# A gated mixer layer on one core: sums of the projections moved from GpSimd to VectorE, and the residual written into the result banks before the output products

## The chip, the cores and the metric

The kernel runs on one core of one Trainium2 chip. A core has TensorE (PE: matrix products out of SBUF into eight PSUM banks of 128 x 512 f32), VectorE (DVE), ScalarE (ACT), GpSimd (POOL) and SyncE (SP, which only issues transfers here). Each engine works through its own queue in order; semaphores connect them. The metric is the device time in microseconds.

## The reference

One layer over 512 tokens of width 1024. What matters here:

```python
h = x @ w_in[i]
ua, va, za, qh, kh, vh, zb, ga, gb = jnp.split(h, IN_OFFSETS, axis=-1)
...
ya = ua * sa.reshape(bn, s_len, A_WIDTH) * jax.nn.silu(za)
...
yb = o.reshape(bn, s_len, B_WIDTH) * jax.nn.silu(zb)
merged = jax.nn.sigmoid(ga) * (ya @ w_branch_a[i]) + jax.nn.sigmoid(gb) * (yb @ w_branch_b[i])
mix_out = merged @ w_out[i]
ple = jax.nn.sigmoid(x @ w_ple_gate[i]) * (p[i] @ w_ple[i])
x = layer_norm(DEEPNORM_ALPHA * x + mix_out + ple, ln_g[i], ln_b[i])
```

`DEEPNORM_ALPHA` is the fourth root of 2, `ALPHA` in the kernel. `w_in`, `w_branch_a`, `w_branch_b`, `w_out` and `w_ple_gate` have 1024 rows, `w_ple` has 256.

## The kernel before

**Products.** An f32 operand is split into a high part (fp32r) and the rest: `h` is a ScalarE copy, `l` is VectorE's `x - h`. Such a pair of operations is called a cut. Each f32 product is then three TensorE products, `three` (L291): high times high, high times low, low times high. A weight unit is 128 x 1024; it is loaded into `wr`, cut into `wh` (L409, ACT) and `wl` (L412, DVE), of which four pairs of buffers rotate.

**Stages.** The projections run one after the other: those of the attention branch first, with the attention beside them, then `ua`, `za`, `va`, `zq`, `ga`, `gb`, `pg` (the embedding's gate), `ple` (the embedding), `wb`, `wa` (the two branch projections) and the output. `va` to `pg`, `wb` and `wa` go through `quad` (L649), which does a 1024 x 1024 product over 2 x 2 blocks with seven block products in place of eight. Its left operand is needed in seven forms: quarters `11`, `12`, `22` and four sums of quarters that the code calls S1, S2, S3 and N4 (a quarter is 512 features by 256 tokens, a tile of 128 x 1024; S1 = 21 - 22, S3 = 11 - 21, S2 = 22 - 11, N4 = S2 + 12). The weights are summed in the same way, by accumulating transfers that POOL issues (L384, in `follow`) when a unit has been cut, or beforehand in memory (`ws_...`). A quad has seven steps of 24 products, in three pairs of banks X, Y and Z. After a step, `after1` to `after7` and `block` (L662) combine banks with ACT copies and DVE subtractions and call the stage's `done`.

**The order around the change.** There is no scheduler. `product` (L279) counts products, and `later(n, fn)` puts `fn` into the program n products further on. Each engine's queue has the order in which such calls fall due; an engine does not wait for a product unless a semaphore says so. The numbers in lines 80 to 92 are such distances: `YB...` and `YA...` say when the quarters and sums of `yb` and `ya` are made and cut, in halves (`in_parts`: two numbers for two halves of 128 x 512). The sums are made by POOL (`add`, L1221 to 1223), the cuts by ACT and DVE (`cut_part`, L1208). `yb`'s are made during `gb` and `pg`, to be there for `wb`; `ya`'s during `pg`, `ple` and `wb`, for `wa`. Their places are the four slots of `ys` (tiles `xsh`, `xsl`), the regions of `xh` and `xl` that `x` no longer needs, and two tiles `yag`, `yab` (`first_sum`) whose room the last norm's gain and shift take later.

**Gates and merge.** `gate_done` (L1195) applies the sigmoid to `ga` and `gb` and stores them in DRAM; `load_gates` brings them back in pairs, through SP, at the distances `GATES`. `mb_done` (L1314) multiplies `wb`'s result by its gate (two of eight pieces on POOL, the others on DVE), `merge` (L1346) does so for `wa` and adds the two (for tokens 0 to 255 on POOL in part). `merge_turn` (L1353) follows at a distance `MERGE`: four TensorE transposes into bank `tr` or `po`, an ACT copy into `xh` and a DVE subtraction into `xl`.

**Embedding, residual and norm.** `base` holds the gate of the embedding, `embed` (L1288) turns it into gate times embedding over `ALPHA`, and `residue` (L1292) adds `x` to it by an accumulating transfer that POOL issues, at the start of the output. The output's first half of the columns is done for two token blocks at a time, with units loaded as it goes, the second half block by block; the last block's second half in two pieces of 256 columns. After each piece `residual` (L1369) adds the bank over `ALPHA` to `base` (DVE) and takes its statistics, and `last_norm` (L1374) normalises and stores; the norm is that of the sum over `ALPHA`, with `EPS` over `ALPHA` squared.

Of the kernel before, what the change touches and what calls it, by code (L numbers as in the profile page):

```python
# [21 lines left out]
P = 128  # L22
# [52 lines left out]

GOES_ON = ('v', 'gb', 'pg', 'wb', 'wa')
# [169 lines left out]
def hybrid_layer(ctx: ExitStack, tc: tile.TileContext, a, out: bass.AP):  # L246
# [402 lines left out]
    def quad(name, left, banks, place, done):  # L649
# [555 lines left out]
    def part_of(tiles, k, t, part):  # L1205
        return (tile[:, 4 * k + 2 * part:4 * k + 2 * part + 2, t * 2 * P:(t + 1) * 2 * P] for tile in tiles)

    def cut_part(source, where, part):  # L1208
        h, l = part_of((xh, xl), *where, part) if where in ((0, 0), (1, 0), (0, 1), (1, 1)) else where(part)
        act.activation(h, source, AF.Copy)  # L1210
        later(CUT_LOW, lambda: dve.tensor_tensor(out=l, in0=source, in1=h.bitcast(F32), op=OP.subtract))

    def cut_yb(k, t, where, part):
        source, = part_of((yb[0],), k, t, part)
        cut_part(source, where, part)

    def cut_ya(k, t, where, part):
        source, = part_of((ua,), k, t, part)
        cut_part(source, where, part)

    def add(tile, to, op, x, y, part):  # L1221
        (z,), (x,), (y,) = (part_of((tile,), *q, part) for q in (to, x, y))
        pool.tensor_tensor(out=z, in0=x, in1=y, op=op)

    def add_ya(*what):
        add(ua, *what)

    def add_yb(*what):
        add(yb[0], *what)
# [6 lines left out]
    def first_sum(part):  # L1236
        if not alone:
            alone.extend(late.tile([P, 4, 2 * P], F32R, name="ya" + n, tag=n) for n in "gb")
        return (tile[:, 2 * part:2 * part + 2, :] for tile in alone)

    def of_first_sum(t, k):
# [25 lines left out]
    in_parts(cut_yb, YB11, 0, 0, (0, 0))  # L1267
    in_parts(cut_yb, YB12, 1, 0, (1, 0))
    in_parts(add_yb, YB_S2, (0, 0), OP.subtract, (1, 1), (0, 0))
    in_parts(add_yb, YB_N4, (1, 0), OP.add, (0, 0), (1, 0))  # L1270
    in_parts(cut_yb, YB_CUT_S1, 1, 1, slot(0))
    in_parts(cut_yb, YB_CUT_N4, 1, 0, slot(2))
    in_parts(cut_yb, YB_CUT_S2, 0, 0, slot(1))
    in_parts(cut_yb, YB_CUT_S3, 0, 1, slot(3))
    in_parts(cut_ya, YA22, 1, 1, (1, 1))
    in_parts(add_ya, YA_S1, (1, 1), OP.subtract, (0, 1), (1, 1))
    in_parts(add_ya, YA_S3, (0, 1), OP.subtract, (0, 0), (0, 1))
    in_parts(cut_ya, YA_CUT_S1, 1, 1, first_sum)
# [49 lines left out]
    in_parts(cut_ya, YA11, 0, 0, (0, 0))  # L1328
    in_parts(cut_ya, YA12, 1, 0, (1, 0))
    in_parts(add_ya, YA_S2, (0, 0), OP.subtract, (1, 1), (0, 0))  # L1330
    in_parts(add_ya, YA_N4, (1, 0), OP.add, (0, 0), (1, 0))
    in_parts(cut_ya, YA_CUT_S3, 0, 1, slot(0))
    in_parts(cut_ya, YA_CUT_N4, 1, 0, slot(2))
    in_parts(cut_ya, YA_CUT_S2, 0, 0, slot(1))
# [11 lines left out]
    def merge(c, t, z, source):  # L1346
        early = t < NT // 2
        by = pool if early and c else dve
        by.tensor_tensor(out=z, in0=source, in1=gate.pop(("ga", c, t)), op=OP.mult)
        (pool if early else dve).tensor_tensor(out=z, in0=z, in1=mb[0][:, t, c * T:(c + 1) * T], op=OP.add)  # L1350
        later(MERGE["early" if early else c], merge_turn, c, t, z)

# [10 lines left out]
    of_ya = [of_first_sum, of_sum(ys, 1), of_sum(ys, 2), of_sum(ys, 0)]  # L1363
    quad("wa", operands(xh, xl, of_ya), pairs(False), lambda c, t: None, merge)


    zst = [small([P, 2 if t < NT - 1 else 3, 6], "vst", 4) for t in range(NT)]

    def residual(t, piece, n, bank):  # L1369
        z = base[:, t, piece * n:(piece + 1) * n]  # L1370
        dve.scalar_tensor_tensor(out=z, in0=bank, scalar=1.0 / ALPHA, in1=z, op0=OP.mult, op1=OP.add)
        dve.bn_stats(out=zst[t][:, piece if n == T else piece - 1, :], in_=z)

    def last_norm(t, cuts):  # L1374
        mv, rs = rstd_of(zst[t], EPS / ALPHA ** 2)
        lg, lb = norm_last
        for c in cuts:
            z = base[:, t, c]
            dve.scalar_tensor_tensor(out=z, in0=z, scalar=mv[:, 0:1], in1=lg[:, c],
                                     op0=OP.subtract, op1=OP.mult)  # L1380
        for c in cuts:
            z = base[:, t, c]
            dve.scalar_tensor_tensor(out=z, in0=z, scalar=rs[:, 0:1], in1=lb[:, c], op0=OP.mult, op1=OP.add)
            sp.dma_start(out=out[t * P:(t + 1) * P, c], in_=z)
# [84 lines left out]
```

## Time and profile before

| what | us |
|---|---|
| median of three runs (lowest, highest) | 621.21 (620.9, 624.6) |
| the profiled execution | 622.56 |
| its span, first to last instruction | 620.8 |
| `pg`: 432.09 to 471.65 | 39.56 |
| `ple`: 471.65 to 482.80 | 11.15 |
| `wb`: 482.80 to 522.38 | 39.58 |
| `wa`: 522.38 to 566.31 | 43.93 |
| output: 566.31 to the last product's end | 47.2 |

Times in the profile count from the first instruction. A row of the timeline has a start, a duration, the engine, the line, the operation, what it writes and reads, how many are merged into it, and in brackets how long the engine had stood still and what ended that. A matmul row's end overlaps the next one's start, so stalls of TensorE are read from start to start. DMA share is the mean busy share of the 16 DMA engines. A tile's name stands without its buffer's number: `ps_pp`, `ps_tx`, `ps_sc`, `ps_tr` and `ps_po` are the banks (three, one, two, one, one).

### The profile page before, as it was taken

How to read it: one execution, taken by the hardware profiler on the slowest of the kernel's cores; microseconds unless marked ns; L12 is line 12 of the kernel's file. 1: busy time of each engine (PE TensorE's matmuls, PEld its weight loads, DVE VectorE, ACT ScalarE, POOL GpSimd, SP SyncE). 2: the span in 40 equal slices, each digit the busy share in tenths (PEclk: the TensorE clock that was granted, in tenths of full speed). 3: DMA queues.
4: the chain of work that ended last, by engine and by line, in shares of the span. 5: the costliest groups of instructions: out<-in, count | busy, mean ns of one | idle time of the engine just before them, and what ended most of it. 6: DMA issues, size and time to landing. Idle time of an engine off the chain costs nothing.

```text
span 620.8 us, 8616 instructions
## 1 busy us (share of the span) xinstructions
PE 607.7 (98%) x3012; PEld 508.5 (82%) x3012; DVE 470.4 (76%) x778; ACT 338.3 (54%) x542; POOL 156.6 (25%) x156
## 2 busy tenths in 40 slices
PE   9999999999999999999999999999999999998995
PEld 6888888888888888888899988888887787776884
DVE  6995687878888765748578987678799788658476
ACT  6656664645645654478665665546676554543200
POOL 1234011332432630230102121141423152443011
PEclk9999999999999999999999999999999999999998
DMA  8789889679797597668898898967976487999102
GB/s 288 237 242 190 259 288 268 246 188 290 267 255 273 177 295 223 160 183 300 272 311 191 244 226 241 234 173 232 232 205 195 178 235 208 255 224 267 33 34 102
DMA packets 45631, 138.52 MB, mean 223 GB/s; under 512 B 6036, under 2 KB 7188, under 8 KB 45268
## 3 DMA queue, kind: packets, MB, share of 16 engines
q1 hardware_dynamic: 35092, 102.71, 46.4%
q0 software_dynamic: 9920, 34.87, 30.7%
q8 instruction: 24, 0.39, 0.3%
q10 hardware_dynamic: 576, 0.39, 0.2%
q14 instruction: 19, 0.16, 0.1%
HBM read 118.95 MB, written 30.54 MB: 241 GB/s over the span
## 4 chain that ended last, share of the span: by engine, by line
PE 85%; DMA 6%; DVE 4%; issue 3%; ACT 1%; POOL 1%; DVEq 0%; SPq 0%; POOLq 0%; ACTq 0%
PE ps_pp L280 52%; PE ps_sc L280 15%; PE ps_tx L280 6%; PE ps_sc L801 3%; DMA wr<-in_w 3%; PE ps_po L846 3%; DMA gates<-gate_ga 1%; DVE wl L412 1%; PE ps_tr L835 1%; PE ps_po L280 1%; PE ps_tr L280 1%; DMA wr<-ws_wb 1%; DVE base L1290 1%; PE ps_tr L1172 1%; PE ps_po L1172 1%
## 5 line engine op out<-in xcount | busy, mean ns | idle before, releaser
L412 DVE TENSOR_TENSOR wl<-wr,wh 128x1024 fp32r<-128x1024 f32 (+1 forms) x143 | 190.2, 1334 | 45.6 <-ACT wh L409 43.4
L409 ACT ACTIVATE wh<-wr 128x1024 fp32r<-128x1024 f32 (+1 forms) x143 | 147.1, 1033 | 72.9 <-PE ps_sc L280 29.0
L280 PE MATMUL ps_pp<-xh,wh 128*128 128x512 f32 (+1 forms) x276 | 109.3, 397 | 0.0
L280 PE MATMUL ps_pp<-xl,wh 128*128 128x512 f32 (+1 forms) x276 | 107.0, 388 | 0.1
L280 PE MATMUL ps_pp<-xh,wl 128*128 128x512 f32 (+1 forms) x276 | 105.5, 383 | 0.0
L280 PE MATMUL ps_pp<-wh,xh 128*128 128x512 f32 (+1 forms) x168 | 64.0, 381 | 0.3 <-DVE s L665 0.2
L280 PE MATMUL ps_pp<-wh,xl 128*128 128x512 f32 (+1 forms) x168 | 64.2, 382 | 0.0
L280 PE MATMUL ps_pp<-wl,xh 128*128 128x512 f32 (+1 forms) x168 | 64.0, 381 | 0.0
L814 ACT ACTIVATE p<-p,sth 128x128 f32<-128x128 f32 (+3 forms) x64 | 35.5, 556 | 46.6 <-DVE sth L812 46.5
L384 POOL DMA_DIRECT2D wr<-in_w x34 | 29.6, 872 | 122.1 <-DVE wl L412 118.1
L280 PEld LDWEIGHTS ps_pp<-xh,wl 128*128 128x128 f32 x276 | 52.1, 189 | 8.9 <-DVE wl L307 0.2
L280 PEld LDWEIGHTS ps_pp<-xh,wh 128*128 128x128 f32 x276 | 52.0, 189 | 8.5 <-ACT wh L306 0.5
L280 PEld LDWEIGHTS ps_pp<-xl,wh 128*128 128x128 f32 x276 | 52.1, 189 | 8.3 <-DVE xl L307 0.4
L746 POOL TENSOR_TENSOR hl<-m,hl 128x512 fp32r<-128x512 f32 x16 | 25.1, 1627 | 54.4 <-ACT hl L741 54.4
L280 PEld LDWEIGHTS ps_pp<-wh,xh 128*128 128x128 f32 x168 | 31.6, 188 | 7.3 <-DVE s L665 0.6
L280 PEld LDWEIGHTS ps_pp<-wl,xh 128*128 128x128 f32 x168 | 31.6, 188 | 6.2 <-DVE wl L412 0.4
L280 PEld LDWEIGHTS ps_pp<-wh,xl 128*128 128x128 f32 x168 | 31.6, 188 | 5.7
L808 DVE CUSTOM_DVE_ANT_0 p<-ps_sc,mask 128x128 f32<-128x128 f32 (+3 forms) x64 | 30.9, 483 | 6.3 <-PE ps_sc L801 6.3
L280 PE MATMUL ps_sc<-wl,xsh 128*128 128x512 f32 x88 | 34.5, 392 | 0.6 <-DVE wl L412 0.6
L280 PE MATMUL ps_sc<-wh,xsh 128*128 128x512 f32 x88 | 34.3, 390 | 0.0
L280 PE MATMUL ps_sc<-wh,xsl 128*128 128x512 f32 x88 | 34.2, 389 | 0.0
L280 PE MATMUL ps_pp<-wh,xsh 128*128 128x512 f32 x80 | 31.4, 393 | 0.1
(315 smaller groups left out, 1268.1 us busy)
## 6 DMA issues: line engine op xcount, KB each, us to landing
wr<-in_w SPq DMA_DIRECT2D x81, 512.0 KB, 4.7
wr<-in_w POOLq DMA_DIRECT2D x30, 512.0 KB, 6.2
k<-hl SPq DMA_DIRECT2D x16, 256.0 KB, 5.4
q<-hl SPq DMA_DIRECT2D x16, 256.0 KB, 4.1
ws_va<-in_w POOLq DMA_DIRECT2D x8, 512.0 KB, 10.3
wr<-ws_va SPq DMA_DIRECT2D x8, 512.0 KB, 4.3
wa<-in_w POOLq DMA_DIRECT2D x6, 512.0 KB, 7.2
kx<-hl SPq DMA_DIRECT2D x12, 256.0 KB, 5.4
```

Source lines behind the costliest of these rows:

```text
L280: pe.matmul(ps, s, m, start=start, stop=stop, skip_group_check=read_within)
L384: pool.dma_start(out=raw[u][:, :n], in_=weights(STEPS[FOLLOWS[u]][1], n), accum_op=OP.add)
L409: act.activation(h, raw[u][:, :width(STEPS[u][0])], AF.Copy)
L412: dve.tensor_tensor(out=l, in0=raw[u][:, :width(STEPS[u][0])], in1=h.bitcast(F32), op=OP.subtract)
L746: pool.tensor_tensor(out=hl[:, 3 - j, :], in0=m[2 * j], in1=hl[:, j, :].bitcast(F32), op=OP.subtract)
L801: pe.matmul(sc[m][:, :n], q[:, m, i * P:(i + 1) * P], kk[:, m, :n], start=o == 0, stop=o == 1)
L808: dve.tensor_tensor_reduce(out=pr[m][:, :n], in0=sc[m][:, :n], in1=mask[:, T - n:], scale=-(DK ** -0.5), scalar=3e38, op0=OP.add, op1=OP.m ...
L814: act.activation(pr[m][:, :n], pr[m][:, :n], AF.Exp, bias=st[:, m:m + 1], scale=-1.0, accum_out=st[:, 2 + m:3 + m])
L835: pe.transpose(tr[:, j * P:(j + 1) * P], ad[:, j * P:(j + 1) * P], ident)
L846: pe.matmul(po[:, i * P:(i + 1) * P], at[:, j * P:(j + 1) * P], v[:, j, h * P:(h + 1) * P], start=j == 0, stop=j == i)
L1172: pe.matmul(sa[:, t * P:(t + 1) * P], va[:, t, g * P:(g + 1) * P], aux[0][:, 0, g, :], start=True, stop=True)
L1290: dve.scalar_tensor_tensor(out=z, in0=bank, scalar=1.0 / ALPHA, in1=z, op0=OP.mult, op1=OP.mult)
```

## The change

- Quarters are cut whole (`split_quarter`), not in halves. Sums of `yb` stay on POOL in halves (a tuple of two distances in `combine`), as do S1 and S3 of `ya`; S2 and N4 of `ya` go to DVE, whole (a single distance).
- S1 and S3 of `ya`, made in `ple` before (distances 180 to 204 from the start of `pg`), are made in `pg`. Quarter `22` of `ya` is cut in `pg` too, into the two tiles apart; the sum S1 takes the place in `xh` and `xl` that the quarter had, and is cut in `wb`. The cut of `yb`'s S3 falls into `wb`, the cuts of `ya`'s N4 and S2 into `wa`.
- `pT` is loaded and cut earlier in `pg`.
- In `ga`, `gb` and `pg` the sigmoid follows its subtraction by 8 products, not 2.
- All multiplications and additions of `mb_done` and `merge` are DVE's. `MERGE` has a distance for each piece.
- The four transfers that add `x` to `base` are issued in `wb`; the loads of the last norm's gain and shift move from `wa` into the output.
- `fill`: ScalarE writes `ALPHA * base` into a result bank, for nine pieces in eight banks; the output's products start without clearing the bank and accumulate onto it. `residual` falls away: `stats` reads the bank, and the first step of `last_norm` reads it in place of `base`. The norm is that of the sum itself.

```diff
+SIGMOIDS = ('ga', 'gb', 'pg')
-YB22, YB_S1, YB_S3 = (60, 72), (80, 92), (104, 116)
-YB11, YB12, YB_S2, YB_N4 = (26, 33), (50, 57), (46, 58), (70, 82)
-YB_CUT_S1, YB_CUT_N4, YB_CUT_S2, YB_CUT_S3 = (75, 82), (101, 108), (124, 131), (150, 157)
-YA22, YA_S1, YA_S3, YA_CUT_S1 = (170, 177), (180, 188), (196, 204), (200, 207)
-YA11, YA12, YA_S2, YA_N4 = (26, 33), (50, 57), (44, 52), (68, 76)
-YA_CUT_S3, YA_CUT_N4, YA_CUT_S2 = (78, 85), (98, 105), (122, 129)
+YB22, YB_S1, YB_S3 = 60, (80, 92), (104, 116)
+YB11, YB12, YB_S2, YB_N4, YB_SUMS = 25, 49, (34, 46), (58, 70), (75, 101, 124, 226)
+YA22, YA_S1, YA_S3 = 36, (84, 96), (108, 120)
+YA11, YA12, YA_S2, YA_N4, YA_SUMS = 26, 50, 54, 64, (19, 76, 172, 196)
-LAST_NORM = (100, 130)
-MERGE = {'early': 24, 1: 23, 0: 22}
-RESIDUE = (2, 8, 26, 32)
+LAST_NORM = (172, 184)
+MERGE = (36, 36, 25, 27), (40, 40, 68, 62)
+RESIDUE = (10, 34, 58, 82)
+FIRST_FILL = (150, 156)
+FILL = ((14, 0, 1), (20, 2, 0), (24, 1, 1), (30, 3, 0), (136, 2, 1), (160, 3, 1), (164, 3, 2))
...
-            later(2, done, c, t, z, z)
+            later(8 if name in SIGMOIDS else 2, done, c, t, z, z)
...
+    def split_quarter(n, source, where):
+        def high():
+            h, l = where()
+            act.activation(h, source, AF.Copy)
+            later(CUT_LOW, lambda: dve.tensor_tensor(out=l, in0=source, in1=h.bitcast(F32), op=OP.subtract))
+
+        later(n, high)
+
+    def combine(ats, to, op, x, y):
+        def part(engine, e):
+            z, a0, a1 = (q[:, e] for q in (to, x, y))
+            engine.tensor_tensor(out=z, in0=a0, in1=a1, op=op)
+
+        if isinstance(ats, int):
+            later(ats, part, dve, slice(0, 4))
+        else:
+            for i, n in enumerate(ats):
+                later(n, part, pool, slice(2 * i, 2 * i + 2))
...
-            later(40 + 12 * k, cut, phl[0][:, 0, k, :], phl[0][:, 1, k, :], pt)
-
-    later(64, load_p)
+            later(26 + 12 * k, cut, phl[0][:, 0, k, :], phl[0][:, 1, k, :], pt)
+
+    later(34, load_p)
...
-        by = pool if c == 1 and t < 2 else dve
-        by.tensor_tensor(out=z, in0=source, in1=gate.pop(("gb", c, t)), op=OP.mult)
+        dve.tensor_tensor(out=z, in0=source, in1=gate.pop(("gb", c, t)), op=OP.mult)
...
+    for t, n in enumerate(RESIDUE):
+        later(n, residue, t)
...
-        early = t < NT // 2
-        by = pool if early and c else dve
-        by.tensor_tensor(out=z, in0=source, in1=gate.pop(("ga", c, t)), op=OP.mult)
-        (pool if early else dve).tensor_tensor(out=z, in0=z, in1=mb[0][:, t, c * T:(c + 1) * T], op=OP.add)
-        later(MERGE["early" if early else c], merge_turn, c, t, z)
+        dve.tensor_tensor(out=z, in0=source, in1=gate.pop(("ga", c, t)), op=OP.mult)
+        dve.tensor_tensor(out=z, in0=z, in1=mb[0][:, t, c * T:(c + 1) * T], op=OP.add)
+        later(MERGE[c][t], merge_turn, c, t, z)
...
+    last_columns = [[(0, T), (T, D)] for _ in range(NT - 1)] + [[(0, T), (T, T + T // 2), (T + T // 2, D)]]
+    held = {}
+
+    def fill(t, i):
+        c0, c1 = last_columns[t][i]
+        bank = (pbank("sc", 2) if (t < 2 and i == 0) or (t >= 2 and i == 1) else
+                pbank("tx", 1) if t == 2 else pp())
+        held[t, i] = bank[:, :c1 - c0]
+        act.activation(held[t, i], base[:, t, c0:c1], AF.Copy, scale=ALPHA)
+
+    for t in range(2):
+        later(FIRST_FILL[t], fill, t, 0)
...
+    def stats(t, piece, bank):
+        dve.bn_stats(out=zst[t][:, piece, :], in_=bank)
+
+    def last_norm(t, cuts):
+        mv, rs = rstd_of(zst[t])
+        lg, lb = norm_last
+        for i, cs in enumerate(slice(*c) for c in last_columns[t]):
+            dve.scalar_tensor_tensor(out=base[:, t, cs], in0=held[t, i], scalar=mv[:, 0:1], in1=lg[:, cs],
+                                     op0=OP.subtract, op1=OP.mult)
...
-    def residual(t, piece, n, bank):
-        z = base[:, t, piece * n:(piece + 1) * n]
-        dve.scalar_tensor_tensor(out=z, in0=bank, scalar=1.0 / ALPHA, in1=z, op0=OP.mult, op1=OP.add)
-        dve.bn_stats(out=zst[t][:, piece if n == T else piece - 1, :], in_=z)
...
-                three(banks[t], xh[:, k, ts], xl[:, k, ts], h[:, m], l[:, m], k == 0, k == KT - 1)
+                three(held[t, 0], xh[:, k, ts], xl[:, k, ts], h[:, m], l[:, m], False, k == KT - 1, True)
...
-            later(2 + 6 * (t % 2), residual, t, 0, T, banks[t])
+            later(2 + 6 * (t % 2), stats, t, 0, held[t, 0])
```

More of the change, by code (lines that the diff above doesn't have):

```diff
@@ L1138, in hybrid_layer, with rstd_of @@
     later(AUX[4], mask_ws)
-    def rstd_of(st, eps=EPS):
+    def rstd_of(st):
         mv = small([P, 2], "mv")
         dve.bn_aggr(out=mv, in_=st)
-        dve.tensor_scalar(out=mv[:, 1:2], in0=mv[:, 1:2], scalar1=eps, scalar2=None, op0=OP.add)
+        dve.tensor_scalar(out=mv[:, 1:2], in0=mv[:, 1:2], scalar1=EPS, scalar2=None, op0=OP.add)
         rs = small([P, 1], "rs")
@@ L1203, in hybrid_layer @@
     ys = xs
[L1205 to L1229, printed above, removed]
+    def quarter(tile, k, t):
+        return tile[:, 4 * k:4 * k + 4, t * 2 * P:(t + 1) * 2 * P]
+    def natural(k, t):
+        return lambda: (quarter(xh, k, t), quarter(xl, k, t))
@@ L1231, in slot @@
     def slot(c):
-        return lambda part: (tile[:, c, 2 * part:2 * part + 2, :] for tile in ys)
+        return lambda: (ys[0][:, c], ys[1][:, c])
     alone = []
[L1236 to L1241, printed above, removed]
-        return tuple(tile[:, k, t * P:(t + 1) * P] for tile in alone)
-    def in_parts(fn, ats, *what):
-        for part, n in enumerate(ats):
-            later(n, fn, *what, part)
@@ L1248, in hybrid_layer, with apart, of_apart @@
-    in_parts(cut_yb, YB22, 1, 1, (0, 1))
-    in_parts(add_yb, YB_S1, (1, 1), OP.subtract, (0, 1), (1, 1))
-    in_parts(add_yb, YB_S3, (0, 1), OP.subtract, (0, 0), (0, 1))
+    def apart():
+        alone.extend(late.tile([P, 4, 2 * P], F32R, name="ya" + n, tag=n) for n in "gb")
+        return alone
+    def of_apart(t, k):
+        return tuple(tile[:, k, t * P:(t + 1) * P] for tile in alone)
+    def split_quarter(n, source, where):
[4 more added lines that the diff above has]
+        later(n, high)
@@ new lines, in combine @@
+    def combine(ats, to, op, x, y):
[7 more added lines that the diff above has]
+                later(n, part, pool, slice(2 * i, 2 * i + 2))
+    yb11, yb12, yb21, yb22 = (quarter(yb[0], k, t) for t in range(2) for k in range(2))
+    ya11, ya12, ya21, ya22 = (quarter(ua, k, t) for t in range(2) for k in range(2))
@@ L1251, in hybrid_layer @@
+    split_quarter(YB22, yb22, natural(0, 1))
+    combine(YB_S1, yb22, OP.subtract, yb21, yb22)
+    combine(YB_S3, yb21, OP.subtract, yb11, yb21)
     quad("gb", of_x, pairs(True), lambda c, t: None, gate_done("gb"))
@@ L1265, in embedding_gate @@
         act.activation(z, source, AF.Sigmoid)
[L1267 to L1278, printed above, removed]
+    split_quarter(YB11, yb11, natural(0, 0))
+    combine(YB_S2, yb11, OP.subtract, yb22, yb11)
+    split_quarter(YB12, yb12, natural(1, 0))
+    combine(YB_N4, yb12, OP.add, yb11, yb12)
+    for n, source, c in zip(YB_SUMS, (yb22, yb12, yb11, yb21), (0, 2, 1, 3)):
+        split_quarter(n, source, slot(c))
+    split_quarter(YA22, ya22, apart)
+    combine(YA_S1, ya22, OP.subtract, ya21, ya22)
+    combine(YA_S3, ya21, OP.subtract, ya11, ya21)
     quad("pg", of_x, pairs(False), lambda c, t: base[:, t, c * T:(c + 1) * T], embedding_gate)
@@ L1327, in hybrid_layer @@
         later(n, load_gates, *what, i % 2)
[L1328 to L1334, printed above, removed]
+    split_quarter(YA_SUMS[0], ya22, natural(1, 1))
+    split_quarter(YA11, ya11, natural(0, 0))
+    combine(YA_S2, ya11, OP.subtract, ya22, ya11)
+    split_quarter(YA12, ya12, natural(1, 0))
+    combine(YA_N4, ya12, OP.add, ya11, ya12)
+    for n, source, c in zip(YA_SUMS[1:], (ya21, ya12, ya11), (0, 2, 1)):
+        split_quarter(n, source, slot(c))
+    for t, n in enumerate(RESIDUE):
+        later(n, residue, t)
     quad("wb", operands(xh, xl, ys, 0), pairs(True), place_b, mb_done)
@@ L1361, in merge_turn @@
                                            in1=xh[:, at[0], at[1]].bitcast(F32), op=OP.subtract))
-    of_ya = [of_first_sum, of_sum(ys, 1), of_sum(ys, 2), of_sum(ys, 0)]
-    quad("wa", operands(xh, xl, of_ya), pairs(False), lambda c, t: None, merge)
-    zst = [small([P, 2 if t < NT - 1 else 3, 6], "vst", 4) for t in range(NT)]
-    def residual(t, piece, n, bank):
-        z = base[:, t, piece * n:(piece + 1) * n]
-        dve.scalar_tensor_tensor(out=z, in0=bank, scalar=1.0 / ALPHA, in1=z, op0=OP.mult, op1=OP.add)
-        dve.bn_stats(out=zst[t][:, piece if n == T else piece - 1, :], in_=z)
@@ L1374, in last_norm @@
[L1374 to L1384, printed above, removed]
@@ L1386, in hybrid_layer @@
-    for t, n in enumerate(RESIDUE):
-        later(n, residue, t)
+    of_ya = (of_parts(xh, xl, 0, 0), of_parts(xh, xl, 4, 0), of_parts(xh, xl, 4, 2 * P),
+             of_sum(ys, 2), of_sum(ys, 1), of_sum(ys, 0), of_apart)
+    last_columns = [[(0, T), (T, D)] for _ in range(NT - 1)] + [[(0, T), (T, T + T // 2), (T + T // 2, D)]]
[6 more added lines that the diff above has]
+        act.activation(held[t, i], base[:, t, c0:c1], AF.Copy, scale=ALPHA)
@@ new lines, in hybrid_layer @@
+    for t in range(2):
+        later(FIRST_FILL[t], fill, t, 0)
+    quad("wa", of_ya, pairs(False), lambda c, t: None, merge)
+    def stats(t, piece, bank):
[6 more added lines that the diff above has]
+                                     op0=OP.subtract, op1=OP.mult)
+        for cs in cuts:
+            z = base[:, t, cs]
+            dve.scalar_tensor_tensor(out=z, in0=z, scalar=rs[:, 0:1], in1=lb[:, cs], op0=OP.mult, op1=OP.add)
+            sp.dma_start(out=out[t * P:(t + 1) * P, cs], in_=z)
@@ L1388, in hybrid_layer @@
+    zst = [small([P, 2 if t < NT - 1 else 3, 6], "vst", 4) for t in range(NT)]
     units = []
+    for n, t, i in FILL:
+        later(n, fill, t, i)
     for those in ((0, 1), (2, 3)):
-        banks = {t: pbank("sc", 2) for t in those} if those[0] else {0: pp(), 1: pbank("tx", 1)}
         for k in range(KT):
@@ L1413, in hybrid_layer @@
         ts = slice(t * P, (t + 1) * P)
-        n = T if t < NT - 1 else T // 2
-        for j in range(T // n):
-            bank = pp()
+        for i, (c0, c1) in enumerate(last_columns[t][1:], 1):
             for k in range(KT):
@@ L1422, in hybrid_layer @@
                 h, l = units[k // 2]
-                m = slice((k % 2) * T + j * n, (k % 2) * T + (j + 1) * n)
-                three(bank[:, :n], xh[:, k, ts], xl[:, k, ts], h[:, m], l[:, m], k == 0, k == KT - 1)
-            later(1, residual, t, T // n + j, n, bank[:, :n])
+                m = slice((k % 2) * T + c0 - T, (k % 2) * T + c1 - T)
+                three(held[t, i], xh[:, k, ts], xl[:, k, ts], h[:, m], l[:, m], False, k == KT - 1, True)
+            later(1, stats, t, i, held[t, i])
         later(1, last_norm, t, [slice(0, D)] if t < NT - 1 else [slice(0, T), slice(T, D)])
```

## The prediction

> **What bounds the kernel now.** I read the page's engine totals first, then busy time by stage, then the matmuls in order of time. Stages are found by counting matmuls back from the last: 216 for the output, 168 each for `wa`, `wb`, `pg`, 48 for `ple`. The stage rows below are, in order, `pg`, `ple`, `wb`, `wa`, output, tail; columns are length, then busy time of PE, PEld, DVE, ACT, POOL, the granted clock, DMA share, GB/s.
>
> ```profile
> span 620.8 us, 8616 instructions
> PE 607.7 (98%) x3012; PEld 508.5 (82%) x3012; DVE 470.4 (76%) x778; ACT 338.3 (54%) x542; POOL 156.6 (25%) x156
> ```
>
> ```profile
> 432.09:471.65 39.56, 39.52 (x178) 32.27 (x176) 33.82 (x35) 28.46 (x42) 9.79 (x9) 1.00 0.84 220
> 471.65:482.80 11.15, 11.15 (x49) 9.04 (x48) 10.99 (x14) 5.32 (x8) 6.08 (x4) 1.00 0.51 166
> 482.80:522.38 39.58, 38.87 (x169) 31.30 (x168) 32.74 (x35) 22.74 (x30) 13.55 (x10) 1.00 0.67 212
> 522.38:566.31 43.93, 41.80 (x190) 33.04 (x188) 30.26 (x30) 20.18 (x25) 18.88 (x17) 1.00 0.96 245
> 566.31:613.50 47.19, 45.65 (x229) 38.34 (x227) 31.91 (x43) 6.99 (x8) 4.57 (x3) 1.00 0.29 75
> 613.50:620.80 7.30, 0.00 (x0) 0.00 (x0) 3.89 (x8) 0.00 (x0) 0.99 (x1) 0.64 0.35 136
> ```
>
> TensorE is the bound, at clock 1.00 in every stage; the change leaves its products as they are, so only its stalls and the tail can be won. Six starts of matmuls take 1.36 us:
>
> ```profile
> 461.10 0.39 PE L280 MATMUL ps_pp<-wl,xsh 128*128 128x512 f32 x1
> ...
> 461.78 0.39 PE L280 MATMUL ps_pp<-wl,xsh 128*128 128x512 f32 x1
> ...
> 462.46 0.39 PE L280 MATMUL ps_pp<-wl,xsh 128*128 128x512 f32 x1
> ```
>
> That is 0.227 us a product, 38.1 us for 168. So `wb` (39.58) holds 1.5 us of stalls. The larger stalls stand in the matmul rows, with what released them in brackets:
>
> ```profile
> 495.05 0.39 PE L280 MATMUL ps_sc<-wh,xsh 128*128 128x512 f32 x1
> 496.04 0.50 PE L280 MATMUL ps_sc<-wl,xsh 128*128 128x512 f32 x1 [0.60 <-DVE wl L412]
> ...
> 536.09 0.39 PE L280 MATMUL ps_sc<-wh,yag 128*128 128x512 f32 x1
> 537.29 0.66 PE L1356 MATMUL ps_po<-ident,s 128*128 128x128 f32 x4 [0.81 <-POOL s L1350]
> 537.70 0.47 PE L280 MATMUL ps_sc<-wl,yag 128*128 128x512 f32 x1
> ...
> 559.12 0.39 PE L280 MATMUL ps_pp<-wl,xh 128*128 128x512 f32 x1
> 560.53 0.66 PE L1356 MATMUL ps_tr<-ident,s 128*128 128x128 f32 x4 [1.03 <-POOL s L1350]
> ...
> 569.04 0.39 PE L280 MATMUL ps_tx<-wl,xh 128*128 128x512 f32 x1
> 570.94 0.66 PE L1356 MATMUL ps_po<-ident,z 128*128 128x128 f32 x4 [1.51 <-DVE xl L1360]
> ```
>
> Start to start, less one product, these lose 0.76, 0.97, 1.18 and 1.67 us. A set of four transposes itself takes 0.41 (537.29 to 537.70) and a little after it. Of `wa`'s excess (43.93 - 38.1 = 5.8), six such sets are about 2.7 and the two POOL stalls 2.15; the remaining 1.0 I count as small stalls. So 1.5 in `wb`, 3.1 in `wa` and 1.7 in the output make 6.3 us that a perfect version could win, and the tail comes on top.
>
> **The change, part by part.**
>
> *Where POOL stops DVE.* These rows pair a POOL operation with the DVE operation that met it:
>
> ```profile
> 412.26 4.25 POOL L1223 TENSOR_TENSOR yb<-yb 128x512 f32<-128x512 f32 x3
> ...
> 490.48 1.29 POOL L1223 TENSOR_TENSOR ua<-ua 128x512 f32<-128x512 f32 x1 [9.43 <-DVE xl L1211]
> ...
> 535.65 2.81 POOL L1350 TENSOR_TENSOR s<-s,mb 128x512 f32<-128x512 f32 x2
> ```
>
> ```profile
> 412.81 4.79 DVE L412 TENSOR_TENSOR wl<-wr,wh 128x1024 fp32r<-128x1024 f32 x1 [2.26 <-ACT wh L409]
> ...
> 458.49 1.21 DVE L412 TENSOR_TENSOR wl<-wr,wh 128x1024 fp32r<-128x1024 f32 x1
> ...
> 490.60 2.26 DVE L412 TENSOR_TENSOR wl<-wr,wh 128x1024 fp32r<-128x1024 f32 x1 [0.26 <-DMA wr<-ws_wb]
> ...
> 535.89 4.80 DVE L412 TENSOR_TENSOR wl<-wr,wh 128x1024 fp32r<-128x1024 f32 x2
> ```
>
> A weight cut takes 1.21 alone; it waited 1.05 for one POOL half, 2.4 for two in a row (two cuts, 4.80), 3.6 for three in a row. So a half that meets DVE costs it about 1.1 to 1.2.
>
> *wb, gain 1.1.* POOL loses four halves of S2 and N4 of `ya` and two multiplications; DVE gets two whole quarters (1.21 each), the two multiplications, and the cuts of S1 of `ya` and S3 of `yb`, which come from the stages before. The whole cuts of N4 and S2 leave `wb` for `wa`. On DVE that is +2 x 1.21 + 2 x 0.69 + 2 x 1.21 - 2 x 1.21 = +3.8. Against it stand the waits that go:
>
> ```profile
> 482.80:522.38 39.58, 19.28 (x14) 1.00 0.67 212
> ...
> 569.59 0.69 DVE L1350 TENSOR_TENSOR z<-z,mb 128x512 f32<-128x512 f32 x1
> ```
>
> The 14 weight cuts of `wb` take 19.28 in place of 14 x 1.21 = 16.9, so 2.3 goes. DVE's 32.74 of 39.58 becomes about 34.2: covered, but the first 80 products hold most of it. Of the 1.5 us of stalls I leave 0.4.
>
> *wa and the start of the output, gain 4.3.* POOL's adds and multiplications leave, eight operations of 0.69 on DVE in their place, each right behind the subtraction that feeds it. The transposes are put 36 and 40 products behind (24 and 23 before), 12 x 0.227 = 2.7 us more, more than the 0.97 and 1.18. The last stall hangs on this:
>
> ```profile
> 559.80 8.95 DMA gates<-gate_ga
> ```
>
> ```profile
> DMA to landing us min/median/max: 8.2/12.1/15.2
> ```
>
> The second row is the four POOL transfers that add `x` to `base`, issued at 560.4 to 562.1, beside that gate. They move to `wb`, and the loads of the norm's gain and shift (SP) behind `wa`; `wa` at DMA share 0.96 loses most of the crowd. With a gate as early as the DVE merge allows and transposes 25 and 27 products behind, I keep 0.5 of 3.1 + 1.7 = 4.8 for small stalls.
>
> *The transfers in wb, 0.* POOL's queue reaches the first three at once after the embedding gates (its queue is not tied to products), then the accumulating load for the last `wb` step, the fourth transfer, and the next accumulating load. Share 0.67 leaves a third of 39.6 us free, 13 us; the cover is that `wb`'s loads run two steps ahead. If the cover is gone, the second accumulating load lands late: bounds 0 and one transfer's spacing, (15.2 - 8.2)/3 = 2.3.
>
> *The seeds, 0.* Nine ScalarE writes into banks, about 0.6 each by the nearest row, replace nine DVE operations:
>
> ```profile
> 525.30 0.58 ACT L672 ACTIVATE ps_pp<-ps_pp 128x512 f32<-128x512 f32 x1 [1.66 <-PE ps_pp L280]
> ```
>
> ACT is busy 6.99 of 47.19 in the output stage. The seeds of a second use (136, 160, 164) wait for the norm of tokens two blocks earlier; what is queued behind on ACT is only the next seed, each 8 or more products (1.8 us) ahead of its use. Between 0 and 1.8 were the norm late; I take 0, as DVE has less to do there.
>
> *The tail, gain 0.36.*
>
> ```profile
> 613.51 0.42 DVE L1371 SCALAR_TENSOR_TENSOR base<-ps_pp,base 128x256 f32<-128x256 f32 x1 [0.18 <-PE ps_pp L280]
> 613.97 0.43 DVE L1372 BATCH_NORM_STATS2 vst<-base 128x6 f32<-128x256 f32 x1
> ...
> 614.77 1.40 DVE L1379 SCALAR_TENSOR_TENSOR base<-base,mv,ln_g 128x512 f32<-128x512 f32 x2
> ```
>
> The residual goes (start to start 0.46). The two normalising operations become three (512, 256, 256 columns, read from banks): one more start, about 0.1.
>
> *pg, loss 2.0.* Here the change puts four more POOL halves (S1, S3 of `ya`, from `ple`) beside the four of `yb`, and nothing of POOL stands between the last three. For POOL's halves and the weight cuts in `pg`:
>
> ```profile
> 432.09:471.65 39.56, 6.61 (x4) 1.00 0.84 220
> ```
>
> ```profile
> 432.09:471.65 39.56, 21.28 (x14) 1.00 0.84 220
> ```
>
> ```profile
> 452.53 3.09 DVE L412 TENSOR_TENSOR wl<-wr,wh 128x1024 fp32r<-128x1024 f32 x1
> ```
>
> ```profile
> 456.34 0.39 PE L280 MATMUL ps_pp<-wl,xsh 128*128 128x512 f32 x1
> ```
>
> The cuts wait 21.28 - 16.9 = 4.3 for four halves. Four more bring DVE from 33.82 to 38.1 or more of 39.56: no reserve. The fifth step's second cut ends at 455.62 and is first read at 456.34, a margin of 0.7. Ahead of it come one more whole cut (1.21, YA22) and two cuts of `pT` (0.69 each, 44 products earlier), 2.6, less some 0.6 of DVE idle time: 1.3 late. Then three halves in a row (3.6, as at 412.81) meet the sixth step, whose second cut ends at 459.70 and is read at 461.78, margin 2.1 + 1.3: with the 2.0 carried in that is 2.2 late. Some halves will meet DVE operations that read a bank, so between 1.3 and 3.5 in sum I take 2.0. Ends: 0, and the four added halves' 4.3 in full plus 1.3, 5.6. `ple` is relieved, but PE does not stall there.
>
> The Trainium skill, page "SBUF — State Buffer", section "SBUF: two separate sides", says that POOL and a DVE operation with two SBUF inputs share one port pair as an exclusive lock for the whole instruction. By that rule every added half costs its full 1.29 where the cuts' rows give about 1.1; four would be 0.8 more and the sum 618.4, an estimate.
>
> *Edits of one answer, 0.* Quarters cut whole in place of two halves save DVE 0.15 each (2 x 0.68 against 1.21), counted above within the margins. The sigmoids of `ga`, `gb` and `pg` come 8 products behind their subtraction, not 2, so ACT no longer stands still for DVE there; PE had no stall over 0.2 us in these stages, and the gates are read a stage later. `pT` is loaded 30 products earlier, ahead of two weight loads in SP's queue; those run a step ahead, and one 512 KB transfer's time, some 4 us, is the price without that cover. `base` must be whole at product 150 of `wa`; the slowest addition of `x` took 15.2 us and is issued more than 60 us before. Statistics and normalisation read banks in place of SBUF: 0.69 for 512 columns either way (L1371 reads a bank at 0.42 for 256, L1372 SBUF at 0.43), so 0, and with 0.1 an operation on either side it would be 0.3 at the tail.
>
> *Sum:* -1.1 - 4.3 + 0 + 0 - 0.36 + 2.0 = -3.8. The profiled execution took 622.56 (span 620.8 and 1.8 around it), 1.35 above the median 621.21 of three runs. So 618.8 for it, 617.4 as a median.
>
> **The rivals.** *pg stays covered* (0 there): 621.2 - 5.8 = 615.4, and 614.3 if the 0.9 of stalls that I keep goes too. For it: DVE idles before `pg`, and the POOL halves may find it reading banks. Against it: the 0.7 margin. *Slower: DVE falls behind in pg.* All eight halves hold it for about 1.1 each and the lateness passes on whole: 5.6 us there give 621.0, all but 0.2 of the gains cancelled; at 1.29 a half with nothing hidden (8 x 1.29 = 10.3, less the 4.3 that is there already, plus the 1.3 of moved cuts, 7.3) it is 622.7. It decides from 5.8 us in `pg`. For it speaks the cut at 412.81, which took 4.79; against it, that DVE idles 5.7 of `pg`'s 39.56 now. *The crowd moves into wb:* 2.3 lost at its last step, 619.7. *The change doesn't do what it says:* transposes still wait, because the last merge waits for its gate, now behind SP's other loads; then 1.7 stays, 619.1.
>
> **How the numbers follow.** My forecast has 0.45, `pg` covered 0.28, DVE behind 0.12, the crowd in `wb` 0.09, the gate 0.06. 617.4 is the first; its own range is 616 to 619.5. The range of 8 in 10 runs from 614.4 to 622.0. About 1% (6.2 us) is what can be told from no change: faster means below 615.0, half of the second case, 0.14; slower means above 627.4, which none of the cases gives, 0.03 for what I don't see; 0.83 between.
>
> **What would show it.** Right: `wb` below 38.7, `wa` below 41 with four sets of transposes, none of them released by POOL; no residual behind the last matmul; `pg` near 41.5 with gaps at its fifth and sixth steps released by weight cuts of three or more us. Wrong: `pg` at 39.6 or less; a gap at `wb`'s last step ended by a POOL transfer; an output matmul that waits for ACT.

## The result and the profile after

The changed kernel takes 625.3 us (median of 13 runs, 623.72 to 627.65) against 621.88 before (13 runs, 620.23 to 625.14): a ratio of 1.0052, 95% interval 1.0033 to 1.0071. It is half a per cent slower; the prediction was 617.4 with a range up to 622.0. The numbers of the experiments below leave out one execution of e5 that took 675.38 at a granted clock of 0.85.

The profiled execution took 627.2, 1.9 above its median, and its span is 4.7 longer than before. These are its totals, and its stages by the same count of matmuls as before (`pg`, `ple`, `wb`, `wa`, output, tail; the columns are length, then busy time of PE, PEld, DVE, ACT, POOL, the granted clock, DMA share, GB/s).

```profile
span 625.5 us, 8563 instructions
PE 609.7 (97%) x3012; PEld 510.9 (82%) x3012; DVE 465.1 (74%) x769; ACT 341.6 (55%) x537; POOL 133.8 (21%) x144
```

```profile
432.56:477.33 44.77, 41.51 (x177) 33.36 (x176) 37.36 (x30) 28.48 (x36) 15.16 (x12) 0.96 0.74 193
477.33:488.49 11.16, 11.16 (x50) 9.04 (x48) 8.13 (x10) 3.56 (x4) 1.76 (x2) 1.00 0.53 159
488.49:530.81 42.32, 39.29 (x169) 31.31 (x168) 30.38 (x31) 21.43 (x25) 4.57 (x6) 1.00 0.87 244
530.81:572.54 41.73, 40.56 (x185) 32.95 (x184) 31.52 (x36) 21.36 (x27) 5.96 (x7) 1.00 0.91 228
572.54:618.47 45.93, 45.90 (x233) 38.81 (x231) 27.58 (x40) 11.96 (x18) 1.66 (x3) 1.00 0.19 67
618.47:625.50 7.03, 0.00 (x0) 0.00 (x0) 3.58 (x8) 0.00 (x0) 0.55 (x1) 0.70 0.23 89
```

| stage | before | after | difference |
|---|---|---|---|
| up to `pg` | 432.09 | 432.56 | +0.5 |
| `pg` | 39.56 | 44.77 | +5.2 |
| `ple` | 11.15 | 11.16 | 0 |
| `wb` | 39.58 | 42.32 | +2.7 |
| `wa` and output | 91.12 | 87.66 | -3.5 |
| tail | 7.30 | 7.03 | -0.3 |

So the last stages gain a little less than was forecast, and `pg` and `wb` lose twice as much. The stretch ahead of `pg` ends between 431.8 and 432.7 in all the profiles, so its 0.5 tells nothing.

In `pg`, POOL first meets two weight cuts at the fifth step: they take 3.68 in place of 2 x 1.21, and TensorE stands still for 0.7:

```profile
454.76 1.60 POOL L1235 TENSOR_TENSOR ua<-ua 128x512 f32<-128x512 f32 x1
```

```profile
454.91 3.68 DVE L413 TENSOR_TENSOR wl<-wr,wh 128x1024 fp32r<-128x1024 f32 x2
```

```profile
456.59 0.39 PE L281 MATMUL ps_pp<-wh,xsh 128*128 128x512 f32 x1
457.51 0.50 PE L281 MATMUL ps_pp<-wl,xsh 128*128 128x512 f32 x1 [0.53 <-DVE wl L413]
```

Then three POOL halves in a row stand against one VectorE cut. First POOL, then DVE, then ACT, from the timeline of the changed kernel:

```profile
458.37 4.08 POOL L1235 TENSOR_TENSOR ua<-ua 128x512 f32<-128x512 f32 x3
```

```profile
458.51 5.04 DVE L1228 TENSOR_TENSOR xsl<-yb,xsh 128x1024 fp32r<-128x1024 f32 x1
463.47 1.21 DVE L413 TENSOR_TENSOR wl<-wr,wh 128x1024 fp32r<-128x1024 f32 x1
```

```profile
465.32 0.63 ACT L1262 ACTIVATE base<-base 128x512 f32<-128x512 f32 x1 [5.73 <-DVE base L666]
```

The cut takes 5.04 where 1.21 is usual: 3.8 for three halves, 1.28 each. This cut is of a sum that only `wb` reads, but a weight cut stands behind it (463.47), and behind that the subtraction that ACT's sigmoid waits for. ACT's queue stands still for 5.73 us, and a copy that frees a bank for TensorE stands behind the sigmoid and one weight cut. TensorE meets both, first the weight cut, then the copy:

```profile
462.90 0.39 PE L281 MATMUL ps_pp<-wh,xsh 128*128 128x512 f32 x1
464.74 0.50 PE L281 MATMUL ps_pp<-wl,xsh 128*128 128x512 f32 x1 [1.45 <-DVE wl L413]
...
465.77 0.39 PE L281 MATMUL ps_pp<-wh,xsl 128*128 128x512 f32 x1
467.43 0.64 PE L281 MATMUL ps_pp<-wh,xsh 128*128 128x512 f32 x1 [1.27 <-ACT s L661]
467.87 0.63 PE L281 MATMUL ps_pp<-wl,xsh 128*128 128x512 f32 x1
```

Start to start, less 0.23, that is 1.6 and 1.4 lost. From 467.43 the starts stand 0.43 apart instead of 0.23, for nine starts, which costs 1.6 more; the window row of that stretch has the granted clock, 0.53, in its column after the engines:

```profile
467.40:470.90 3.50, 3.47 (x9) 2.72 (x10) 3.49 (x5) 2.40 (x3) 0.00 (x0) 0.53 0.18 46
```

The three stalls and the slow starts, 0.7 + 1.6 + 1.4 + 1.6 = 5.3, are the 5.2 by which `pg` is longer.

In `wb` the transfers of `x` are in the way twice. Early on, the first three delay a gate; the chain of waits names the gate's 10.91 us, and DVE stands still for it:

```profile
488.73 10.91 DMA gates<-gate_gb
```

```profile
499.76 0.69 DVE L1309 TENSOR_TENSOR mb<-ps_pp,gates 128x512 f32<-128x512 f32 x1 [1.64 <-DMA gates<-gate_gb]
```

From there to 507.9 DVE works without a pause, so it stays late, and TensorE waits for two of its weight cuts, 0.7 each time:

```profile
500.73 0.39 PE L281 MATMUL ps_sc<-wh,xsh 128*128 128x512 f32 x1
501.64 0.50 PE L281 MATMUL ps_sc<-wl,xsh 128*128 128x512 f32 x1 [0.52 <-DVE wl L413]
...
507.02 0.39 PE L281 MATMUL ps_sc<-wh,xsh 128*128 128x512 f32 x1
507.92 0.50 PE L281 MATMUL ps_sc<-wl,xsh 128*128 128x512 f32 x1 [0.51 <-DVE wl L413]
```

At the end the fourth (L1287) stands in POOL's queue between the two accumulating weight loads (L385) of the last step. The second of these is the one that ACT, and then TensorE, wait for:

```profile
509.87 0.88 POOL L385 DMA_DIRECT2D wr<-in_w  x1 [20.37 <-DVE wl L413]
510.99 0.89 POOL L1287 DMA_DIRECT2D base<-in_x  x1 [0.25 <-issue]
512.14 0.89 POOL L385 DMA_DIRECT2D wr<-in_w  x1 [0.25 <-DMA wr<-in_w]
```

```profile
524.45 2.95 ACT L410 ACTIVATE wh<-wr 128x1024 fp32r<-128x1024 f32 x3 [5.36 <-DMA wr<-in_w]
```

```profile
523.92 0.39 PE L281 MATMUL ps_pp<-wh,xl 128*128 128x512 f32 x1
525.55 0.51 PE L281 MATMUL ps_pp<-wh,xh 128*128 128x512 f32 x1 [1.25 <-ACT wh L410]
526.82 0.51 PE L281 MATMUL ps_pp<-wl,xh 128*128 128x512 f32 x1 [0.76 <-DVE wl L413]
```

Issued at 512.14, used from 524.45: 12.3 us for a load whose kind landed in 5.4 and 6.4 in this place before. TensorE loses 1.4 and 1.0 by it. And the tail, where the residual is gone and three operations read the banks:

```profile
618.48 0.43 DVE L1374 BATCH_NORM_STATS2 vst<-ps_pp 128x6 f32<-128x256 f32 x1 [1.57 <-PE ps_pp L281]
...
619.29 0.74 DVE L1380 SCALAR_TENSOR_TENSOR base<-ps_pp,mv,ln_g 128x512 f32<-128x512 f32 x1
619.95 0.48 DVE L1380 SCALAR_TENSOR_TENSOR base<-ps_sc,mv,ln_g 128x256 f32<-128x256 f32 x1
620.34 0.48 DVE L1380 SCALAR_TENSOR_TENSOR base<-ps_pp,mv,ln_g 128x256 f32<-128x256 f32 x1
```

### The profile page after: what moved, and what is told of

It is laid out like the page before. It is cut to its first block, busy times and chain, and to the rows that moved or that the text cites. A ratio compares the mean times of both kernels' runs of the same rounds, so it can differ in the third digit from the quotient of the medians.

```text
span 625.5 us, 8563 instructions
## 1 busy us (share of the span) xinstructions
PE 609.7 (97%) x3012; PEld 510.9 (82%) x3012; DVE 465.1 (74%) x769; ACT 341.6 (55%) x537; POOL 133.8 (21%) x144
## 4 chain that ended last, share of the span: by engine, by line
PE 84%; issue 5%; DMA 5%; DVE 4%; ACT 1%; POOL 0%; DVEq 0%; POOLq 0%; ACTq 0%; SPq 0%
PE ps_pp L281 50%; PE ps_sc L281 15%; PE ps_tx L281 7%; DMA wr<-in_w 3%; PE ps_sc L802 3%; PE ps_po L847 3%; DMA gates<-gate_gb 2%; PE ps_tr L836 1%; DVE wl L413 1%; PE ps_po L281 1%; PE ps_tr L281 1%; DVE xsl L1228 1%; PE ps_po L485 1%; PE ps_tr L1173 1%; PE ps_po L1173 1%
## 5 line engine op out<-in xcount | busy, mean ns | idle before, releaser
L413 DVE TENSOR_TENSOR wl<-wr,wh 128x1024 fp32r<-128x1024 f32 (+1 forms) x143 | 181.3, 1276 | 46.4 <-ACT wh L410 46.0
L385 POOL DMA_DIRECT2D wr<-in_w x34 | 29.8, 876 | 150.4 <-DVE wl L413 148.1
L281 PE MATMUL ps_pp<-wh,xh 128*128 128x512 f32 (+1 forms) x144 | 55.3, 384 | 1.2 <-ACT wh L410 1.2
L281 PE MATMUL ps_pp<-wl,xh 128*128 128x512 f32 (+1 forms) x144 | 55.4, 385 | 0.8 <-DVE wl L413 0.8
L281 PE MATMUL ps_pp<-wh,xl 128*128 128x512 f32 (+1 forms) x144 | 55.4, 384 | 0.0
L281 PE MATMUL ps_pp<-wl,xsh 128*128 128x512 f32 x80 | 32.2, 403 | 2.0 <-DVE wl L413 2.0
L281 PEld LDWEIGHTS ps_pp<-wh,xh 128*128 128x128 f32 x144 | 27.1, 188 | 6.8 <-ACT wh L410 1.7
L281 PEld LDWEIGHTS ps_pp<-wl,xh 128*128 128x128 f32 x144 | 27.1, 188 | 6.3 <-DVE wl L413 1.1
```

What stands on the lines that cost most here:

```text
L281: pe.matmul(ps, s, m, start=start, stop=stop, skip_group_check=read_within)
L385: pool.dma_start(out=raw[u][:, :n], in_=weights(STEPS[FOLLOWS[u]][1], n), accum_op=OP.add)
L413: dve.tensor_tensor(out=l, in0=raw[u][:, :width(STEPS[u][0])], in1=h.bitcast(F32), op=OP.subtract)
```

## The experiments

All were timed beside the kernel before on the same chip: 621.73 for e1, e2, e3 and e5, 622.28 for e6 to e9, 621.89 for e10 and e11. Ratios are to that kernel, with 95% intervals. The stage rows below are from each one's profile.

**What pg loses: the lock or the load.** e1 takes both out of `pg`, e2 only the lock, and gives DVE more to do there.

```diff
 e1
-YA22, YA_S1, YA_S3 = 36, (84, 96), (108, 120)
+YA22, YA_S1, YA_S3 = 170, (180, 188), (196, 204)
 e2 (a single distance: DVE, whole)
+YA22, YA_S1, YA_S3 = 36, 90, 112
```

> S1 and S3 of ya, and the cut that they wait for, go back from pg into ple; all else as changed. Both theories of pg's loss, that the three POOL halves in a row hold VectorE (the lock) and that VectorE has too much work ahead of pg's fifth step (the load), give pg near 39.9 us (44.8 as changed), no stretch at a granted clock of half, and a median about 5 below the changed kernel's 625.3: 620.3. If neither is right, pg stays over 43.

> S1 and S3 of ya stay in pg, but VectorE makes them, whole, at 1.2 us each: its work in pg grows by 2.4 us, the four POOL halves go. The lock gives pg near 40.5 to 41.5 and a median about 4 below 625.3: 621.5. The load gives pg at 46 or more and a median of 627.

e1: 619.43, ratio 0.9953 (0.9937 to 0.9969). e2: 618.84, ratio 0.9948 (0.993 to 0.9967). `pg` of e1, then of e2:

```profile
432.40:471.39 38.99, 38.99 (x177) 32.43 (x176) 31.49 (x29) 28.06 (x35) 10.00 (x8) 1.00 0.84 218
```

```profile
431.85:471.93 40.08, 39.50 (x177) 32.28 (x176) 34.42 (x32) 28.52 (x36) 10.01 (x8) 1.00 0.80 214
```

In e2 DVE does two quarters more than in the changed kernel, and its busy time in `pg` falls from 37.36 to 34.42, as the time that POOL's halves hold it counts as busy. `pg` shortens by 4.7 though DVE has more work: the load theory falls, the lock stands. The three stalls are gone in e2, and one of 0.7 (466.35) is left. By their medians the two kernels gain 5.9 and 6.5 us on the changed one, while `pg` is 5.8 and 4.7 shorter in the profiles; e2 gains in `wb` too, which takes 40.11 there.

**What wb loses: the crowd or DVE's work.** e3 leaves the addition of `x` out, so its result is not the layer's; e5 moves only the fourth transfer.

```diff
 e3
-    for t, n in enumerate(RESIDUE):
-        later(n, residue, t)
 e5
-RESIDUE = (10, 34, 58, 82)
+RESIDUE = (10, 34, 58, 90)
```

> The addition of x to base is left out (four transfers of 512 KB). If these transfers make wb's loss (crowd), wb falls from 42.3 to about 39.3, without a stall at its last step, and the median to 622.3. If VectorE's sums and merges make it (work), wb stays over 41.5 and the median over 624.5.

> Only the fourth transfer of x moves, behind the second accumulating weight load in POOL's queue in place of ahead of it. Crowd: the stalls of 1.4 and 1.0 us at wb's last step go, wb near 40.2, median 623.1; the stalls behind the first three transfers (0.7 and 0.7) stay. Work: nothing changes, 625.3.

e3: 621.77, ratio 0.9994 (0.9977 to 1.0011). e5: 623.45, ratio 1.0021 (0.9999 to 1.0043). `wb` of e3, then of e5:

```profile
489.06:527.16 38.10, 38.10 (x169) 31.53 (x168) 30.21 (x32) 21.65 (x25) 3.50 (x4) 1.00 0.74 223
```

```profile
487.16:527.03 39.87, 38.70 (x169) 31.38 (x168) 30.28 (x31) 21.67 (x25) 5.29 (x6) 1.00 0.93 259
```

Without the transfers `wb` takes 38.10, which is its 168 products and nothing else, with all of DVE's added sums and multiplications in place. So all 4.2 us that `wb` takes beyond its products come from the transfers, and one place in POOL's queue is worth 2.4 of them in e5. That size belongs to the changed kernel's timing: e1 and e2 leave the fourth transfer where it is, the second accumulating load takes 10.4 us to land in both (12.2 in the changed kernel, 7.1 in e5), and TensorE loses 0.6 and 0.7 at that step.

**Where else the transfers could stand.** e6 and e9 put all four behind the accumulating loads; e7 and e9 let DVE make the two sums at the end of `pg` and in `ple`; e11 spreads the transfers over `wb` and `wa`.

```diff
 e6, e9
+RESIDUE = (90, 91, 92, 93)
 e7
+RESIDUE = (10, 34, 58, 90)
 e11
+RESIDUE = (10, 34, 90, 208)
 e6
+YA22, YA_S1, YA_S3 = 36, 90, 112
 e7, e9, e11
+YA22, YA_S1, YA_S3 = 36, 160, 178
```

> As e2 (VectorE makes S1 and S3 of ya), and all four transfers of x stand behind the second accumulating weight load of wb in POOL's queue. If the crowd is only a matter of where the transfers stand, wb falls from 40.1 to about 38.4 and the median from 618.8 to 617.1. If they only shift the crowd, wa grows by what wb wins (its first accumulating loads follow), and the median stays at 618.8.

> VectorE makes S1 and S3 of ya, whole, but in the last products of pg and in ple (160 and 178), and the fourth transfer stands behind the accumulating loads. If pg's last stall under e2 (0.7) is VectorE's work there, pg falls from 40.1 to about 39.1 and wb by some 0.6; median 617.3. If it is something else, 618.8 less at most 0.6.

> e7 with all four transfers behind the accumulating loads, as in e6. Both effects add: pg 39.1, wb 38.3, median about 616.3; if the crowd only shifts, 617.5 to 618.

> e7 with the four transfers of x spread: two behind ple, one behind wb's accumulating loads, one behind the second pair of wa's. Crowd: wb's stall of 0.7 goes and wa keeps its 40.7, median 617.0. If a transfer among wa's accumulating loads costs what it costs in e6, wa grows by 2 or more and the median is over 619.

e6: 627.81, ratio 1.007 (1.0039 to 1.01). e9: 626.32, ratio 1.0058 (1.0041 to 1.0076). Both expectations missed: `wb` is as hoped (38.10 and 38.11), and `wa` is 9.5 us longer than in e2 (e6) and 11.0 longer than in e7 (e9). In e6 the four transfers were issued from 507.0 to 509.0 and took 10.5 to 20.1 us to land. The last gate of `wb`, issued at 517.11 when none of them had landed, landed 16 us later. Its chain of waits, its TensorE rows and its `wa`:

```profile
517.11 16.13 DMA gates<-gate_gb
```

```profile
526.96 0.39 PE L281 MATMUL ps_pp<-wh,xl 128*128 128x512 f32 x1
534.75 0.79 PE L281 MATMUL ps_pp<-wh,xh 128*128 128x512 f32 x1 [7.41 <-ACT ps_pp L673]
```

```profile
521.74:571.51 49.77, 42.10 (x186) 34.06 (x184) 32.25 (x38) 21.72 (x27) 5.24 (x6) 0.93 0.89 232
```

TensorE waits for an ACT copy at `wa`'s second step; by the chain that goes back to DVE, which stands at the multiplication with the late gate. e7 is the best version: 617.66, ratio 0.9913 (0.9882 to 0.9944), 0.9% faster than the kernel before. Its `pg`, `wb` and `wa`:

```profile
431.86:471.70 39.84, 39.38 (x177) 32.27 (x176) 33.53 (x31) 28.27 (x36) 9.97 (x8) 1.00 0.83 217
...
482.86:521.99 39.13, 38.61 (x170) 31.38 (x168) 30.27 (x31) 21.68 (x25) 5.29 (x6) 1.00 0.93 263
521.99:562.65 40.66, 40.49 (x186) 32.96 (x184) 31.56 (x36) 21.72 (x27) 5.24 (x6) 1.00 0.90 234
```

Its `pg` is 0.7 longer than was expected: the stall at the sixth step is gone, and another of 0.6 stands at the fourth. e11: 618.28, ratio 0.9927 (0.9899 to 0.9955), between the two expectations. `wb` is free of stalls, and `wa` is 2.3 longer than in e7. That the fourth transfer does this is not shown: the two larger stalls, 1.3 and 0.9, stand at the same places in `wa` of e10 below (1.2 and 0.9), which has no transfer of `x` there. The `wb` and `wa` of e11:

```profile
482.17:520.28 38.11, 38.11 (x170) 31.53 (x169) 30.11 (x31) 21.66 (x25) 4.39 (x5) 1.00 0.89 256
520.28:563.24 42.96, 40.87 (x186) 32.87 (x185) 31.51 (x36) 21.48 (x27) 6.14 (x7) 1.00 0.93 235
```

**The merges by themselves.** e8 is the kernel before with `mb_done`, `merge` and `MERGE` as changed; e10 adds the transfers' place in `wb`.

```diff
 e8, on the kernel before
+MERGE = (36, 36, 25, 27), (40, 40, 68, 62)
...
-        by = pool if c == 1 and t < 2 else dve
-        by.tensor_tensor(out=z, in0=source, in1=gate.pop(("gb", c, t)), op=OP.mult)
+        dve.tensor_tensor(out=z, in0=source, in1=gate.pop(("gb", c, t)), op=OP.mult)
...
-        (pool if early else dve).tensor_tensor(out=z, in0=z, in1=mb[0][:, t, c * T:(c + 1) * T], op=OP.add)
-        later(MERGE["early" if early else c], merge_turn, c, t, z)
+        dve.tensor_tensor(out=z, in0=z, in1=mb[0][:, t, c * T:(c + 1) * T], op=OP.add)
+        later(MERGE[c][t], merge_turn, c, t, z)
 e10, on e8 (in wb, not in the output)
-RESIDUE = (2, 8, 26, 32)
+RESIDUE = (10, 34, 58, 90)
```

> The kernel before with one part of the change: wb's and wa's gate multiplications and merge additions on VectorE, and the changed distances of the transposes. The prediction's term: the stalls of 0.97, 1.18 and 1.67 that POOL's additions and the late gate made go, wa and output together 4 shorter, median about 617.9. If that gain came from the transfers of x leaving the output instead, the late gate stays, the gain is about 2 and the median 619.8.

> e8 with one more part of the change: the four transfers of x are issued in wb, the fourth behind the second accumulating weight load. If e8 lost its 7.7 us because POOL, freed of the merges, reached these transfers 17 us earlier and the gate's load drowned among them, that stall goes: wa and output together about 4 shorter than in the kernel before, wb up to 1.5 longer, median 619 to 620. If VectorE's merges themselves are late, a stall of some us stays before the first late transposes and the median is over 622.

e8: 627.85, ratio 1.0084 (1.0054 to 1.0113), 5.6 us slower than before where both readings had a gain. In e8 the transfers of `x` are written at the same place as before, but POOL has no merges ahead of them any more and issues them from 543.0, not from 560.4. The view of that line gives their time to landing (before: 8.2, 12.1, 15.2), the chain of waits the gate behind them, and the matmul rows what TensorE lost:

```profile
L1293 POOL DMA_DIRECT2D base<-in_x x4: 1229/1760/2289, 543.0 to 544.6; - x4
...
DMA to landing us min/median/max: 15.9/20.7/25.6
```

```profile
558.24 14.26 DMA gates<-gate_ga
```

```profile
566.23 0.39 PE L280 MATMUL ps_pp<-wl,xh 128*128 128x512 f32 x1
574.16 1.08 PE L1353 MATMUL ps_po<-ident,z 128*128 128x128 f32 x4 [7.54 <-DVE z L1347]
```

7.7 us are lost before one set of transposes. With the transfers in `wb` (e10) the stall is gone: 619.39, ratio 0.9945 (0.9921 to 0.997). Its `wa` and output:

```profile
521.77:564.33 42.56, 40.72 (x185) 32.96 (x184) 29.05 (x34) 18.64 (x23) 5.96 (x7) 1.00 0.97 247
564.33:610.30 45.97, 45.91 (x233) 38.80 (x231) 32.58 (x46) 8.65 (x11) 4.57 (x3) 1.00 0.10 37
```

88.5 against 91.1 before. So the merges on DVE are worth having only together with another place for the transfers. Moving the transfers without the merges was not run.

## Why the prediction was wrong

- *The bound* was read rightly: apart from the tail, what was won or lost is gaps between matmuls, and for 3.5 us the clock. The output stage takes 45.91 to 45.97 us in the changed kernel, e2, e7 and e10.
- *pg, loss 2.0:* the mechanism was right as far as it went. The two stalls that the text worked out, 1.3 at the fifth step and 2.2 at the sixth, measured 0.7 and 1.6, so 2.3 against the 2.0 taken; the three halves were priced at 3.6 and held DVE for 3.8. The step that failed is that lateness was followed only into the next weight cut. The text did not ask who else stands behind the held operation: ACT's sigmoid waited 5.73 for the subtraction behind it, and a bank's copy behind that sigmoid stopped TensorE again (1.4). The 8 products (1.8 us) that the change puts between subtraction and sigmoid did not cover it. The slow clock behind these gaps, 1.6, stood in no term. That the loss of 5.2 is near the upper end given, 5.6, is luck: that end was added up from the holds and the moved cuts alone.
- The rule of the Trainium skill weighed there (page "SBUF — State Buffer", section "SBUF: two separate sides": the pair is held for the whole instruction) agrees better than the estimate of 1.1 a half: 1.28 a half here, where a half by itself takes 1.29 (the POOL row at 490.48). The cut at 412.81 fits it too: it came 0.55 after POOL had begun and waited 3.58 of the 3.70 left, and the one at 458.51 came 0.14 after and waited 3.83 of the 3.94 left.
- *The transfers in wb, 0:* wrong, 4.2 by e3. The step that failed is the cover: a third of the stage's transfer time was free on average, and only the weight loads' two steps of lead were looked at. The gate, issued beside the first three transfers, had no such lead. The accumulating loads were named with a bound of 2.3, and 2.4 was lost there, the sign that the text gave for being wrong.
- *wb, gain 1.1:* the gain was there: without the transfers `wb` takes 38.10, 1.5 below before. The working had DVE busy for 34.2 us; it was 30.4, less than the 32.7 before.
- *wa and output, gain 4.3:* 3.5 in the profile. No transposes wait for POOL or for the late gate; one stall of 0.9, at `wa`'s second step, is an ACT copy, and one of 0.6 stands at its last step.
- *The seeds, 0, and the tail, -0.36:* right; no matmul of the output waits for ACT, and the tail got 0.27 shorter, as the three normalising operations of 0.74, 0.48 and 0.48 take a little longer than the two.
- *The range:* two rivals of the list happened together, DVE behind in `pg` and the crowd in `wb`. Their chances were taken as if one excluded the other, so no case had the sum of both: at the prices given, 621.0 and 2.3, it would have been 623.3, past 622.0.
- *Slips that change nothing:* 615.4 less 0.9 is 614.5, not 614.3, and 617.4 plus 0.8 is 618.2, not 618.4. The fourth transfer was issued 54 us before the first seed read `base`, not more than 60.

## What to carry to other kernels

Work taken off an engine also takes away the delay that its queue gave to the transfers behind it: e8 left every transfer at its place in the program and lost 7.7 us to them. When an operation may be held, price everything queued behind it on its engine and then behind those who wait for that, not only the operation's own reader. And where two unknown costs lie in different stages, the range needs their sum.

## What the runs showed of the hardware

Behind the gaps of 1.6 and 1.4 in `pg` TensorE ran at a granted clock of 0.53 for 3.5 us, nine starts 0.43 apart. The Trainium skill, page "TensorE: Matmul & The Clock Gate", section "What's actually happening", gives half the clock after an idle window of about 3.4 us and the full clock after about as much work. The 3.4 us from 467.43 to 470.86 agree. No single gap was that long here: in the 4.5 us before, matmuls were busy for 1.8. The same section of the Trainium skill calls the window free-running, and the same gaps did not always bring it: in e5 `pg` had them too, at clock 1.00, and took 44.22. So of the 1.6 us that the slow starts cost, about 0.6 shows as a difference between the two: in e5 TensorE waits 0.7 for DVE at 470.42, where the changed kernel has no gap. That the slow clock let DVE catch up there is likely, but no run shows it alone.
